# An unused tile of 640 bytes a partition in front of the FFN's tiles in SBUF

## The chip, the core and the metric

The kernel runs on one core of a Trainium2 chip, as one launch. The metric is the device time in microseconds of one execution. The profile is of a further execution of the same program; its instructions are timed by the hardware profiler, and its span runs from the first instruction's start to the last one's end.

## The reference, cut to what matters

Two layers over a residual stream x of 512 tokens by 1024 features, in float32. Each layer is an FFN at half weight, a mixing step with three groups of attention heads, and a second FFN at half weight:

```
for layer in range(2):
    h = modulate(rmsnorm(x), sh1, sc1)
    x = x + 0.5 * g1 * swiglu(h, w1[layer,0], w3[layer,0], w2[layer,0])
    ... mixing: projections, three kinds of attention, out projection
    h = modulate(rmsnorm(x), sh3, sc3)
    x = x + 0.5 * g3 * swiglu(h, w1[layer,1], w3[layer,1], w2[layer,1])
swiglu(h, w1, w3, w2) = (silu(h @ w1) * (h @ w3)) @ w2      # 1024 -> 2816 -> 1024
```

So there are four FFNs. The modulation (sh, sc, g) is computed from a conditioning vector with the weights `w_ada`.

## The kernel before, in words

Everything is kept with features on the 128 partitions and the 512 tokens along the free axis. To keep float32 accuracy on TensorE, each operand is split in two halves of type fp32r: a rounded part ("h" in `hh`, `gh`, `whi`) and the rest ("l" in `hl`, `gl`, `wlo`). A product of a block of weights (128 x 128, stationary) with a block of activations (128 x up to 512, moving) is then three matmuls that add up in PSUM (`mm3`, lines 309 to 311):

```
mm(out, l[0], r[0], start=start, stop=False, **kw)     # whi with hh or gh   L309
mm(out, l[0], r[1], start=False, stop=False, **kw)     # whi with hl or gl   L310
mm(out, l[1], r[0], start=False, stop=stop, **kw)      # wlo with hh or gh   L311
```

Weights come in pieces of 128 x 1024 float32 (eight blocks) through SyncE's DMA queue into `raw` (three buffers); ScalarE rounds a piece into `whi` (line 271) and VectorE subtracts for `wlo` (line 281), each with five buffers. They run ahead of TensorE until no buffer is free.

An FFN (function `ffn`) runs over two halves of 11 chunks of the 2816 hidden features. In the first part of a half, 8 blocks of w1 and 8 of w3 for each chunk go against the normed input `hh`, `hl` (eight chunks each). Silu and the product give `gf`, and ScalarE and VectorE split it into `gh` and `gl`. In the second part, for each of the eight chunks m of the output, the 11 blocks of w2 go against the 11 `gh`, `gl` of this half:

```
for j in range(HALF):
    wt = self.weight("ffn_w2", (l, f), hf * HALF + j, col(m))
    self.mm3(ps, wt, g[j], j == 0, j == HALF - 1)
```

The moving operand is 512 tokens wide, but in the second half's last two output chunks it is 256 wide (function `products`), so that the next norm can begin early. So an FFN has 14 whole output chunks (eight in the first half, six in the second) x 11 blocks x 3 = 462 matmuls of 512 columns on `gh` or `gl`, and 2 x 11 x 3 x 2 = 132 of 256 columns; the four FFNs have 1848 and 528.

Where the tiles lie in SBUF is settled when the program is built: pools are laid one behind the other, and a pool that is closed gives its room to the next. The constants, the weights (`raw`, `whi`, `wlo`), the activations (`hh`, `hl`) and small tiles come first and stay for the whole program. Behind them, from byte 113600 of each partition, lies either the FFN's pool (`fp`, opened by `open_ffn`) or the mixing's pool (`mp`). The FFN's pool holds `nt` (temporary of the norms), `sil`, `gf`, `gh`, `gl`, and, for the conditioning, `adaw` and `silc`. Byte addresses in a partition, as the built programs have them:

| tile | before | after | start modulo 512 before, after |
|---|---|---|---|
| `whi`, five of 4096 bytes | 36416 on | the same | 64, 64 (and each block of 128 columns in them) |
| `wlo`, five of 4096 bytes | 56896 on | the same | 64, 64 (and each block) |
| `hh`, eight of 2048 bytes | 77376 on | the same | 64, 64 |
| `hl`, eight of 2048 bytes | 93760 on | the same | 64, 64 |
| `gh`, fourteen at a time of 2048 bytes | 125888 on | 126528 on | 448, 64 |
| `gl`, fourteen at a time of 2048 bytes | 154560 on | 155200 on | 448, 64 |
| `nt`, `sil`, `gf`, `adaw`, `silc` | from 113600 | from 114240 | 448, 64 |
| `qk`, `att`, `tf` of the mixing's pool, `rmat` | 161344, 185920, 142912, 19520 on | the same | 64, 64 |

Modulo 2048 the tiles `hh`, `hl` start at 1600; `gh` and `gl` start at 960 before and at 1600 after.

Of the kernel before, what the change touches and what calls it, by code (L numbers as in the profile page):

```python
# [26 lines left out]
P = 128  # L27
# [36 lines left out]
def unit_sbuf(t, u):  # L64
# [4 lines left out]
SMALL = [("norm_g", (DEPTH * 3, KC), True),  # L69
         ("b_ada", (DEPTH, NMOD, KC), True), ("out_g", (DEPTH, KC), False), ("qk_g", (DEPTH, 4, RD), False),  # L70
         ("qk_gcol", (DEPTH, 4), False), ("rope", (2, NT, RD), False)]
HT = S // 2
HALVES = [slice(0, HT), slice(HT, S)]
TAIL = 2
# [108 lines left out]
class Net:  # L183
# [354 lines left out]

    def open_ffn(self, es):
        self.fp = es.enter_context(self.tc.tile_pool(name=self.name("fp"), bufs=1))  # L540
        self.temp = lambda: self.t(self.fp, "nt", [P, S], bufs=6)

    def open_ada(self):
# [112 lines left out]
    def unit_out(self, pair, u, z, att):  # L656

        nc = self.nc
        heads = range(2) if u == 0 else (u - 1,)
        outs = {e: z[:, HT * i:HT * i + HT] for i, e in enumerate(heads)}  # L660
        for i, (e, c, _, o, w) in enumerate(KEY_UNITS[u]):
            lhs = self.v[pair][:, c, e].rearrange("p a b -> p (a b)")
            for j, a in enumerate(att):
                nc.tensor.matmul(outs[e][:, HT - w:], lhs, a[:, o:o + w], start=i + j == 0,  # L664
                                 stop=c == KEY_UNITS[u][-1][1] and j == 1, skip_group_check=True)
# [3 lines left out]
        for e in heads:  # L669
            out = self.o[pair][HD * e:HD * e + HD, HT * (u > 0):HT * (u > 0) + HT]  # L670
            own, other = (outs[e][HD * i:HD * i + HD] for i in (e, 1 - e))
# [336 lines left out]
    def out_last(self, l):  # L1008
# [3 lines left out]
        for cs in HALVES:  # L1012
# [3 lines left out]
            order = [(c, m) for g in range(2) for c in range(4) for m in range(4 * g, 4 * g + 4)]  # L1016
            ps = lambda m: zs[m // 4][:, m % 4 * HT:m % 4 * HT + HT]
            for c, m in order:
# [140 lines left out]
```

## Time and profile before

| | |
|---|---|
| median of 3 runs | 2143.43 us (2143.17 to 2144.86) |
| the profiled execution: its own time | 2149.0 us |
| its span, first to last instruction | 2147.1 us |
| TensorE (PE) busy | 2096.4 us, 98% of the span |
| VectorE (DVE), ScalarE (ACT) busy | 60%, 39% |
| granted TensorE clock, mean | 0.996 of full speed |

The ends of matmuls in the profile are modelled, since they run in a pipeline: a row's duration for a matmul is longer than the time in which the next one follows. What a matmul costs in a stream of them is read as the distance from one start to the next, in the timeline. "PEld" rows are the loads of the stationary operand, which overlap the matmul before.

### The profile page before, as it was taken

What the parts mean: (1) busy time and instruction counts of PE and PEld (TensorE: products, weight loads), DVE (VectorE), ACT (ScalarE), POOL (GpSimd) and SP (SyncE); (2) the same over time, 40 slices, a digit from 0 to 9 for tenths busy, and PEclk for the clock granted to TensorE, in tenths of its full rate; (3) what the DMA queues carried; (4) which work ended last, traced back from release to release, by engine and by line L of the source; (5) the groups of instructions that cost most, each with busy time, mean ns of one, the idle gap of its engine ahead of it and who ended that gap; (6) DMA issues with size and microseconds to landing.
All of it is one profiled execution on the core that took longest, in us unless ns stands there. A gap on an engine that the chain in (4) does not pass through costs nothing.

```text
span 2147.1 us, 28606 instructions
## 1 busy us (share of the span) xinstructions
PE 2096.4 (98%) x11280; PEld 1806.7 (84%) x11280; DVE 1289.2 (60%) x2425; ACT 837.4 (39%) x1347; POOL 3.5 (0%) x12
## 2 busy tenths in 40 slices
PE   6999999999999999999999999999999999999999
PEld 5888888888998888888898888888889998888888
DVE  8772753679978777275374333346899776333332
ACT  3321222467675432122242222324776644222220
POOL 0000000000000000000000000000000000000000
PEclk9999999999999999999999999999999999999999
DMA  7783853342333378386334333324334223333331
GB/s 297 264 283 98 265 171 89 103 107 67 100 91 103 112 262 279 98 269 199 90 105 132 98 98 96 93 82 122 91 84 106 74 71 108 98 89 99 98 102 56
DMA packets 86149, 281.74 MB, mean 131 GB/s; under 512 B 10752, under 2 KB 13312, under 8 KB 86016
## 3 DMA queue, kind: packets, MB, share of 16 engines
q1 hardware_dynamic: 84576, 277.83, 42.3%
q8 instruction: 88, 1.44, 0.3%
q10 hardware_dynamic: 1440, 2.10, 0.3%
q14 instruction: 45, 0.37, 0.1%
HBM read 256.55 MB, written 2.10 MB: 120 GB/s over the span
## 4 chain that ended last, share of the span: by engine, by line
PE 84%; DVE 10%; ACT 3%; DMA 2%; issue 1%; SPq 0%; ACTq 0%; DVEq 0%
PE z L309 23%; PE z L311 23%; PE z L310 23%; PE b L309 3%; PE b L311 3%; PE b L310 3%; DVE sc L862 2%; DVE m L861 2%; PE z L620 1%; DVE att L575 1%; DMA qk<-qk 1%; DVE wlo L281 1%; PE z L664 1%; PE z L713 1%; DVE tf L725 1%
## 5 line engine op out<-in xcount | busy, mean ns | idle before, releaser
L281 DVE TENSOR_TENSOR wlo<-raw,whi 128x1024 fp32r<-128x1024 f32 (+1 forms) x338 | 412.4, 1221 | 534.0 <-ACT whi L271 532.0
L271 ACT CAST whi<-raw 128x1024 fp32r<-128x1024 f32 (+1 forms) x338 | 354.3, 1049 | 863.1 <-PE z L310 791.8
L309 PE MATMUL z<-hh,whi 128*128 128x512 f32 (+1 forms) x1616 | 597.6, 371 | 6.9 <-DVE xs L996 3.9
L310 PE MATMUL z<-hl,whi 128*128 128x512 f32 (+1 forms) x1616 | 597.5, 370 | 0.5
L311 PE MATMUL z<-hh,wlo 128*128 128x512 f32 (+1 forms) x1616 | 596.4, 370 | 1.3 <-DVE wlo L281 1.3
L309 PEld LDWEIGHTS z<-hh,whi 128*128 128x128 f32 x1616 | 306.4, 190 | 59.1 <-DVE xs L996 4.3
L311 PEld LDWEIGHTS z<-hh,wlo 128*128 128x128 f32 x1616 | 306.3, 190 | 52.6 <-DVE wlo L281 1.8
L310 PEld LDWEIGHTS z<-hl,whi 128*128 128x128 f32 x1616 | 306.5, 190 | 52.0 <-DVE hl L437 1.3
L309 PE MATMUL z<-gh,whi 128*128 128x512 f32 (+1 forms) x792 | 293.7, 371 | 0.0
L310 PE MATMUL z<-gl,whi 128*128 128x512 f32 (+1 forms) x792 | 292.9, 370 | 0.0
L311 PE MATMUL z<-gh,wlo 128*128 128x512 f32 (+1 forms) x792 | 289.2, 370 | 0.0
L356 DVE CUSTOM_DVE_ANT_0 adaw<-adaw,silc 128x1024 f32<-128x1024 f32 x144 | 170.9, 1222 | 30.0 <-DMA adaw<-in_w_ada_dram 29.9
L309 PEld LDWEIGHTS z<-gh,whi 128*128 128x128 f32 x792 | 148.9, 188 | 29.7
L311 PEld LDWEIGHTS z<-gh,wlo 128*128 128x128 f32 x792 | 149.0, 188 | 27.7
L310 PEld LDWEIGHTS z<-gl,whi 128*128 128x128 f32 x792 | 149.0, 188 | 26.5
L309 PE MATMUL b<-whi,hh 128*128 128x256 f32 x544 | 156.7, 288 | 3.0 <-DVE v L654 2.1
L311 PE MATMUL b<-whi,hl 128*128 128x256 f32 x544 | 154.7, 284 | 0.0
L310 PE MATMUL b<-wlo,hh 128*128 128x256 f32 x544 | 154.6, 284 | 0.0
L513 DVE SCALAR_TENSOR_TENSOR xs<-z,mod,xs 128x512 f32<-128x512 f32 (+1 forms) x72 | 49.7, 691 | 124.7 <-PE z L311 124.6
L309 PEld LDWEIGHTS b<-whi,hh 128*128 128x128 f32 x544 | 104.8, 193 | 4.0 <-PE b L311 2.4
L310 PEld LDWEIGHTS b<-wlo,hh 128*128 128x128 f32 x544 | 104.8, 193 | 0.2
L311 PEld LDWEIGHTS b<-whi,hl 128*128 128x128 f32 x544 | 104.6, 192 | 0.0
(146 smaller groups left out, 2242.9 us busy)
## 6 DMA issues: line engine op xcount, KB each, us to landing
raw<-in_w_dram SPq DMA_DIRECT2D x332, 512.0 KB, 3.6
adaw<-in_w_ada_dram SPq DMA_DIRECT2D x144, 512.0 KB, 4.8
qk<-qk SPq DMA_DIRECT2D x144, 128.0 KB, 2.3
qk<-qk SPq DMA_DIRECT2D x24, 96.0 KB, 3.3
xs<-in_x_dram SPq DMA_DIRECT2D x4, 512.0 KB, 5.2
raw<-in_w_dram SPq DMA_DIRECT2D x4, 492.0 KB, 3.5
silc<-in_c_dram SPq DMA_DIRECT2D x3, 512.0 KB, 5.1
out_dram<-xs ACTq DMA_DIRECT2D x6, 256.0 KB, 2.0
```

The costliest lines, as they stand in the source:

```text
L271: nc.scalar.copy(hi[:, :n], raw[:, :n])
L281: self.nc.vector.tensor_sub(lo[:, :n], raw[:, :n], hi.bitcast(F32)[:, :n])
L309: mm(out, l[0], r[0], start=start, stop=False, **kw)
L310: mm(out, l[0], r[1], start=False, stop=False, **kw)
L311: mm(out, l[1], r[0], start=False, stop=stop, **kw)
L356: r = self.nc.vector.tensor_tensor_reduce(w, w, self.silc, 1.0, 0.0, op0=ALU.mult, op1=ALU.add, accum_out=m[:, j:j + 1])
L513: nc.vector.scalar_tensor_tensor(self.x[m][:, cs], ps[:, cs], gate[:, m:m + 1], self.x[m][:, cs], op0=ALU.mult, op1=ALU.add)
L575: nc.vector.tensor_sub(unit_sbuf(lo, u), src, unit_sbuf(hi.bitcast(F32), u))
L620: self.nc.tensor.matmul(out, a, b, start=start and i == 0, stop=stop and i == 1, skip_group_check=True)
L664: nc.tensor.matmul(outs[e][:, HT - w:], lhs, a[:, o:o + w], start=i + j == 0, stop=c == KEY_UNITS[u][-1][1] and j == 1, skip_group_check=True)
L861: nc.vector.max(m8, sc)
L862: nc.vector.match_replace(sc, m8, sc, TAKEN)
```

## The change

One tile `shift` of 160 float32 a partition (640 bytes) is allotted as the first tile of the FFN's pool each time that this pool is opened. Nothing writes or reads it. Every other tile of that pool so lies 640 bytes higher; all tiles of the other pools stay where they are. The built programs have on each engine the same instructions in the same order with the same semaphore waits; they differ in the addresses of the FFN pool's tiles alone. The pool ends at byte 208448 at most, where it ended at 207808 before, so it still fits.

```diff
+SHIFT = 160
 ...
     def open_ffn(self, es):
         self.fp = es.enter_context(self.tc.tile_pool(name=self.name("fp"), bufs=1))
+        self.t(self.fp, "shift", [P, SHIFT])
         self.temp = lambda: self.t(self.fp, "nt", [P, S], bufs=6)
```

## Rows read from the trace of the kernel before

**Rows 1.** The page's first part: busy time, share of the span, instructions.

```profile
span 2147.1 us, 28606 instructions
PE 2096.4 (98%) x11280; PEld 1806.7 (84%) x11280; DVE 1289.2 (60%) x2425; ACT 837.4 (39%) x1347; POOL 3.5 (0%) x12
```

**Rows 2.** The page's chain that ended last, shares of the span by engine, by line.

```profile
PE 84%; DVE 10%; ACT 3%; DMA 2%; issue 1%; SPq 0%; ACTq 0%; DVEq 0%
```

**Rows 3.** Groups by line and shape: xcount, then busy us and mean ns.

```profile
L310 PE MATMUL z<-hl,whi 128*128 128x512 f32 x1296 | 505.3, 390 | 0.0
...
L310 PE MATMUL z<-gl,whi 128*128 128x512 f32 x616 | 243.2, 395 | 0.0
...
L310 PE MATMUL z<-gl,whi 128*128 128x256 f32 x176 | 49.6, 282 | 0.0
```

**Rows 4.** Timeline of PE in a first part: start us, duration us, instruction.

```profile
904.71 0.39 PE L309 MATMUL z<-hh,whi 128*128 128x512 f32 x1
904.94 0.39 PE L310 MATMUL z<-hl,whi 128*128 128x512 f32 x1
...
910.83 0.39 PE L309 MATMUL z<-hh,whi 128*128 128x512 f32 x1
```

**Rows 5.** Timeline of PE at both ends of a second part.

```profile
838.64 0.39 PE L310 MATMUL z<-hl,whi 128*128 128x512 f32 x1
838.86 0.39 PE L311 MATMUL z<-hh,wlo 128*128 128x512 f32 x1
839.09 0.40 PE L309 MATMUL z<-gh,whi 128*128 128x512 f32 x1
839.32 0.39 PE L310 MATMUL z<-gl,whi 128*128 128x512 f32 x1
839.55 0.40 PE L311 MATMUL z<-gh,wlo 128*128 128x512 f32 x1
839.79 0.39 PE L309 MATMUL z<-gh,whi 128*128 128x512 f32 x1
840.01 0.40 PE L310 MATMUL z<-gl,whi 128*128 128x512 f32 x1
...
892.65 0.39 PE L311 MATMUL z<-gh,wlo 128*128 128x512 f32 x1
892.88 0.40 PE L309 MATMUL z<-hh,whi 128*128 128x512 f32 x1
```

**Rows 6.** Busy time by stretch: stretch, length, engines (xcount), granted clock, DMA share, GB/s.

```profile
842.00:892.00 50.00, 50.00 (x217) 40.35 (x216) 20.56 (x25) 10.07 (x10) 0.00 (x0) 1.00 0.46 152
904.00:1020.00 116.00, 116.00 (x513) 96.06 (x512) 71.66 (x104) 33.27 (x41) 0.00 (x0) 1.00 0.69 226
```

**Rows 7.** Waits in 839 to 893 us: us in total, times, longest.

```profile
ACT whi L271 <- PE z L310: 42.7, 10, 6.7
DVE wlo L281 <- ACT whi L271: 19.2, 7, 5.1
DVE xs L513 <- PE z L311: 9.0, 4, 3.5
DVE adaw L356 <- DMA adaw<-in_w_ada_dram: 1.7, 2, 1.1
```

**Rows 8.** Timeline of PE in the 256-wide tail of a second half.

```profile
1067.66 0.28 PE L309 MATMUL z<-gh,whi 128*128 128x256 f32 x1
...
1069.91 0.28 PE L310 MATMUL z<-gl,whi 128*128 128x256 f32 x1
```

**Rows 9.** Timeline of PE in the out projection, 256 wide on `hh`, `hl`.

```profile
695.82 0.28 PE L309 MATMUL z<-hh,whi 128*128 128x256 f32 x1
...
698.46 0.28 PE L310 MATMUL z<-hl,whi 128*128 128x256 f32 x1
```

**Rows 10.** Timeline of PE in the mixing: merged rows and the row behind each.

```profile
434.87 0.98 PE L620 MATMUL z<-qk,qk 128*128 128x512 f32 x4
435.69 0.28 PE L309 MATMUL b<-whi,hh 128*128 128x256 f32 x1
...
586.06 1.16 PE L713 MATMUL z<-att,rmat 128*128 128x512 f32 x6
587.05 0.33 PE L309 MATMUL b<-whi,hh 128*128 128x256 f32 x1
```

**Rows 11.** Groups by line and shape on VectorE and ScalarE.

```profile
L437 DVE SCALAR_TENSOR_TENSOR hl<-nt,mod,hh 128x256 fp32r<-128x256 f32 x64 | 27.3, 481 | 2.2 <-ACT hh L436 2.1
...
L437 DVE SCALAR_TENSOR_TENSOR hl<-tf,mod,hh 128x256 fp32r<-128x256 f32 x16 | 6.9, 481 | 2.9 <-ACT hh L436 2.9
```

**Rows 12.** The page's DMA issues: xcount, KB each, median us to landing.

```profile
raw<-in_w_dram SPq DMA_DIRECT2D x332, 512.0 KB, 3.6
adaw<-in_w_ada_dram SPq DMA_DIRECT2D x144, 512.0 KB, 4.8
```

## The prediction

> **What bounds the kernel now.** I read the page's busy times first: TensorE is busy for 98% of the span, VectorE for 60%, ScalarE for 39% [rows 1]. The chain that ended last says the same: 84% of it is TensorE, 10% VectorE [rows 2]. So time that TensorE gains or loses in a long stretch of matmuls is, almost whole, time of the kernel. The stretch that concerns this change is the second part of each half of an FFN, where `gh` and `gl` stream against the w2 blocks, since these two are the only tiles of the FFN's pool that TensorE reads there. Its waits [rows 7] name nobody whom TensorE waits for: ScalarE and VectorE wait for TensorE to free `whi`, 42.7 us of 54, and the weights are there ahead of it.
>
> Next I looked at what one matmul costs. The groups by shape already show a difference that the code does not explain: 512 columns on `hl` have a mean of 390 ns, 512 columns on `gl` have 395 [rows 3]. The ends of these rows are modelled, so I went to the timeline and took distances from start to start. In a first part, on `hh` and `hl`: from 904.71 to 910.83 us are 27 steps, 6.12 / 27 = 226.7 ns each [rows 4]. In a second part, on `gh` and `gl`: from 839.09 to 892.88 us are 231 steps (all of them on `gh` or `gl`), 53.79 / 231 = 232.9 ns each [rows 5]. The change of pace falls on the very first `gh`: 838.64 to 838.86 to 839.09 are the regular steps, and then come 0.23, 0.23, 0.24, 0.22 in turn, which go on to the end.
>
> What could make two matmuls of equal shape differ by 6.2 ns? [...] The other engines don't explain it: in the first part VectorE is busy for 71.66 of 116 us and the DMA engines for 0.69, in the second for 20.56 of 50 us and 0.46, and the slower matmuls stand in the quieter stretch [rows 6]. The order in `mm3`, the stationary tiles and the PSUM tile `z` are the same. What remains is where the moving operand lies: `hh` and `hl` start at the same remainder modulo 512 bytes as every weight block (64), `gh` and `gl` at 448.
>
> **The change part by part.** No instruction, no wait and no transfer is added, removed or moved, so there is nothing to price but the addresses.
>
> *TensorE, 512 columns.* After the change `gh` and `gl` start at 64 modulo 512, and at 1600 modulo 2048, as `hh` and `hl` do. Their matmuls are then of the same form, with the same remainders, as those of [rows 4]. The trace has no `gh` at that place; the nearest row is `hh` at 226.7 ns, and it is near, since only the higher address bits differ. The eight `hh` and the five `whi` and `wlo` buffers already meet in many distances of whole 512 bytes without a change of pace. The gain is 1848 x (232.9 - 226.7) = 11.5 us. Its bounds: all of it, or nothing, if the place is not the cause.
>
> *TensorE, 256 columns.* Here the trace points the other way. In the tail `gh` runs from 1067.66 to 1069.91 us in 19 steps, 118.4 ns each [rows 8]; the out projection's `hh` from 695.82 to 698.46 in 22 steps, 120.0 ns each [rows 9]. If the tail takes the pace of `hh`, it loses 528 x 1.6 = 0.8 us. Its bounds are 0 and 0.8, and I take the loss.
>
> *VectorE and ScalarE.* Instructions that read a tile of the FFN's pool together with another (`nt` with `hh`) meet the new place too. The same line runs in the mixing with its temporary `tf`, which lies at 64 modulo 512 where `nt` lies at 448: both have 481 ns [rows 11]. So I price these at 0, with 0 on both sides.
>
> *DMA.* Only `adaw` and `silc` are loaded into that pool. `adaw` lands in 4.8 us where `raw`, as large and at remainder 64, needs 3.6 [rows 12]; that could be its place or its being issued in bursts. It is hidden either way: VectorE's waits for it are 1.7 us in 54 [rows 7], VectorE is off the path there, and the weights' loads are ahead. I take 0.
>
> *Sum.* 11.5 - 0.8 = 10.7 us less. The profiled execution took 2149.0 us with a span of 2147.1 [rows 1], 5.6 us above the median of the runs. The gain is a number of matmuls times a distance and doesn't hang on which execution one takes, so I subtract it from the median: 2143.4 - 10.7 = 2132.7 us, 0.50% less. Nothing else takes the bound over: in the first parts the same weights chain feeds TensorE at 226.7 ns a matmul while VectorE also does the conditioning, so it can feed the second parts at that pace.
>
> [...] The row says that equal shapes, at an equal clock, differ by 6.2 ns with the tile that is streamed [rows 4, 5]. [...]
>
> **The rivals.**
>
> *Place is not the cause (no change).* Something else in the second part, such as 11 blocks into one bank instead of 8, makes the matmuls slower, and stays: 2143.4 us. The onset at the first `gh` [rows 5] fits this too, as that is where the second part begins. Against it is that the uneven steps begin with the second matmul on `gh`, long before a group of 11 blocks is over. That equal remainders are not enough is a second form of it: four score products on `qk`, which lies at 64 like its stationary tile, take from 434.87 to 435.69 us [rows 10] for 1792 columns; at the pace of `hh` (13.3 ns over the columns' time) they would take 0.80, so each has about 5 ns more. If `gh` stayed 5 ns above `hh`, the gain would be 1848 x 1.2 = 2.2 us: 2141.2. Against this form is that those are short runs of mixed widths, and `gh` runs 198 or more in a row at one width.
>
> *Partial.* The irregular steps get shorter, but not to 226.7; halfway is a gain of 5.7 us: 2137.7.
>
> *Slower.* [...] The worst rows for operands at equal remainders are the stick-breaking products on `att` and `rmat`: six of 2048 columns together from 586.06 to 587.05 us [rows 10], 0.99 where 0.93 would be the pace of `hh`, about 9.5 ns more each. If `gh` ran so, 512 columns would cost 236.2 and 256 columns 129.5 ns: 1848 x 3.3 + 528 x 11.1 = 12.0 us more, 2155.4. It decides from a distance of 232.9 ns on. Against it are all the `hh` rows.
>
> **How the numbers follow.** 0.2% (4.3 us) is about what a measurement of this kernel can tell from no change. My forecast with the full pace of `hh` has 0.79, the partial one 0.06 (faster by over 0.2%, mostly), no change in either form 0.11, slower 0.04. So faster 0.85, same 0.11, slower 0.04. The predicted time is 2132.7. Around it the runs scatter by about 1 us, and the two terms may be off by some 10%. A range from 2130.0 up to the partial case, 2138.0, leaves out less than 2 in 10.
>
> **What the changed kernel's profile would show.** Right: in the second parts the steps on `gh` and `gl` are 226.7 ns and regular, the mean of the 512-column groups on `gl` falls from 395 to 390, the 256-column tail goes from 118.4 to 120, each half of an FFN with 264 such matmuls ends 1.6 us earlier against its start, and no group outside TensorE changes its mean by more than a few ns. Wrong: if the steps stay at 229 to 238 in turn, the place was not the cause; if they settle in another irregular rhythm, the remainder modulo 512 doesn't tell the whole; if they are regular and the kernel is not faster, something that I took as hidden came up, and the first place to look is what ends TensorE's idle time between the parts.

## The result and the profile after

| | before | after |
|---|---|---|
| median | 2144.14 us (4 runs, 2143.17 to 2145.4) | 2133.73 us (4 runs, 2131.62 to 2134.43) |
| the profiled execution, span | 2147.1 us | 2132.2 us |

The ratio is 0.9949 with a 95% interval of 0.9932 to 0.9967: the change makes the kernel 0.5% faster, by 10.4 us. In a second comparison (five runs of the change and nine of the kernel before) it was 2135.85 against 2145.74 us, ratio 0.9951 [0.9939, 0.9964], 9.9 us. The forecast was 2132.7.

The diff puts three lines into the file, so line 309 of before is 311 after, 310 is 312, 437 is 439. First the groups by line and shape of the changed kernel, the lines that answer to [rows 3] and [rows 11]; the columns are count, busy us and mean ns.

```profile
L312 PE MATMUL z<-hl,whi 128*128 128x512 f32 x1296 | 505.1, 390 | 0.0
...
L312 PE MATMUL z<-gl,whi 128*128 128x512 f32 x616 | 239.9, 390 | 0.0
...
L312 PE MATMUL z<-gl,whi 128*128 128x256 f32 x176 | 49.8, 283 | 0.0
...
L439 DVE SCALAR_TENSOR_TENSOR hl<-nt,mod,hh 128x256 fp32r<-128x256 f32 x64 | 27.3, 480 | 2.3 <-ACT hh L438 2.2
```

The group on `gl` went from 395 to 390 ns, the mean that `hl` has, and `hl` stayed. VectorE's instruction on `nt`, whose tile moved too, has 480 ns where it had 481.

Next the timeline of PE in the changed kernel around the start of the second part that [rows 5] shows for before, and 28 steps of the same part (start us, duration us, instruction).

```profile
832.14 0.39 PE L312 MATMUL z<-hl,whi 128*128 128x512 f32 x1
832.37 0.39 PE L313 MATMUL z<-hh,wlo 128*128 128x512 f32 x1
832.59 0.39 PE L311 MATMUL z<-gh,whi 128*128 128x512 f32 x1
832.82 0.39 PE L312 MATMUL z<-gl,whi 128*128 128x512 f32 x1
833.04 0.39 PE L313 MATMUL z<-gh,wlo 128*128 128x512 f32 x1
...
833.95 0.39 PE L311 MATMUL z<-gh,whi 128*128 128x512 f32 x1
...
840.30 0.39 PE L312 MATMUL z<-gl,whi 128*128 128x512 f32 x1
```

The first `gh` no longer breaks the pace: the steps go on as on `hh`. From 833.95 to 840.30 us are 28 steps, 226.8 ns each, where [rows 5] had 232.9.

One execution can mislead about the sum. The two spans differ by 14.9 us, half as much again as the medians. Here are stretches in which the granted clock was 0.50 or 0.51 in the profile of before, and then stretches near three of them in the profile of after (stretch, length, busy time of PE, PEld, DVE, ACT, POOL, granted clock, DMA share, GB/s).

```profile
397.00:400.40 3.40, 3.40 (x16) 3.39 (x15) 3.40 (x10) 2.34 (x6) 0.00 (x0) 0.51 0.40 146
458.50:461.90 3.40, 3.40 (x12) 2.92 (x11) 0.97 (x2) 1.87 (x2) 0.00 (x0) 0.50 0.32 72
717.90:721.30 3.40, 3.40 (x17) 3.40 (x18) 3.40 (x9) 1.95 (x5) 0.00 (x0) 0.50 0.01 5
```

```profile
396.00:400.00 4.00, 4.00 (x29) 4.00 (x28) 3.74 (x11) 3.01 (x6) 0.00 (x0) 1.00 0.04 11
457.00:461.00 4.00, 4.00 (x24) 3.35 (x22) 3.91 (x10) 2.04 (x3) 0.00 (x0) 1.00 0.01 4
716.00:721.00 5.00, 4.19 (x33) 3.74 (x33) 3.79 (x16) 0.00 (x0) 0.00 (x0) 1.00 0.35 108
```

The profile of before has five such stretches of 3.4 us at half clock, that of after two. In the stretch from 717.90 us the steps of 256 columns on `hh` and `hl` took 213 ns, where their mean over the whole profile is 119.9; in the one from 458.50 us 512 columns took 427 ns, where those on `hh` have 226.8. By these ratios 3.4 us at half clock did the work of 1.8 to 1.9 us, so, while TensorE is what the kernel waits for, the three that are missing are worth some 4.6 us, an estimate. 14.9 - 4.6 = 10.3 us is left, about what the medians show. The number of these stretches was between one and five in all profiles of this study, with and without a faster `gh`: four in the first experiment below, three and two in others of the same speed. It is scatter and no gain of the change. Runs of equal clock say the same: in the second comparison the four runs of the change with a mean granted clock of 0.998 took 2133.7 to 2135.9 us, and the two runs of the kernel before with that clock 2145.0 and 2145.2 us.

### The profile page after: what moved, and what is told of

It is laid out like the page before. It is cut to its first block, busy times and chain, and to the rows that moved or that the text cites. A ratio compares the mean times of both kernels' runs of the same rounds, so it can differ in the third digit from the quotient of the medians.

```text
span 2132.2 us, 28606 instructions
## 1 busy us (share of the span) xinstructions
PE 2081.8 (98%) x11280; PEld 1800.9 (84%) x11280; DVE 1288.7 (60%) x2425; ACT 837.7 (39%) x1347; POOL 3.0 (0%) x12
## 4 chain that ended last, share of the span: by engine, by line
PE 83%; DVE 12%; ACT 3%; DMA 2%; issue 1%; SPq 0%; ACTq 0%; DVEq 0%
PE z L311 23%; PE z L313 23%; PE z L312 23%; PE b L311 3%; PE b L313 3%; PE b L312 3%; DVE sc L865 2%; DVE m L864 2%; DVE wlo L283 2%; DVE att L578 1%; PE z L623 1%; PE z L667 1%; DMA qk<-qk 1%; DVE tf L728 1%; ACT tf L770 1%
## 5 line engine op out<-in xcount | busy, mean ns | idle before, releaser
L273 ACT CAST whi<-raw 128x1024 fp32r<-128x1024 f32 (+1 forms) x338 | 354.8, 1050 | 852.1 <-PE z L312 782.5
L311 PE MATMUL z<-hh,whi 128*128 128x512 f32 (+1 forms) x1616 | 596.7, 370 | 7.0 <-DVE xs L999 3.9
L311 PEld LDWEIGHTS z<-hh,whi 128*128 128x128 f32 x1616 | 305.6, 189 | 59.1 <-ACT hh L438 4.4
L311 PE MATMUL z<-gh,whi 128*128 128x512 f32 (+1 forms) x792 | 291.1, 368 | 0.0
L311 PEld LDWEIGHTS z<-gh,whi 128*128 128x128 f32 x792 | 149.3, 189 | 27.5 <-DVE xs L515 0.7
L311 PE MATMUL b<-whi,hh 128*128 128x256 f32 x544 | 156.5, 288 | 3.0 <-DVE v L657 2.1
L311 PEld LDWEIGHTS b<-whi,hh 128*128 128x128 f32 x544 | 104.6, 192 | 4.0 <-PE b L313 2.4
```

What stands on the lines that cost most here:

```text
L273: nc.scalar.copy(hi[:, :n], raw[:, :n])
```

## The experiments

The question for all of them is how long a step (start to start) on `gh`, `gl` and on `hh`, `hl` is, and what sets it. The mean step is worked out from the timeline of each run: all distances between successive starts on these tiles, without those over 60 ns above the columns' own time (waits). That own time is put at 0.417 ns a column, an estimate from `hh`'s paces in [rows 4] and [rows 9]: (226.7 - 120.0) / 256; it leaves 13.3 ns a matmul. "Distance" is the moving tile's start minus the stationary block's start, modulo 256 bytes; that 256 is the right number is what the runs with 384 and 256 bytes showed.

| kernel | distance of `gh` | `gh`, 512 wide | `gh`, 256 wide | `hh`, 512 wide | time, us |
|---|---|---|---|---|---|
| before | 128 | 232.8 ns (1844 steps) | 118.9 ns (516) | 226.8 ns (3876) | 2144.1 |
| the change, 640 bytes | 0 | 227.2 | 119.8 | 226.7 | 2133.7 |
| weights moved to `gh` | 0 | 227.2 | 119.8 | 226.7 | 2135.4 |
| 128 bytes | 0 | 227.1 | 119.8 | 226.7 | 2135.6, one run |
| 384 bytes | 0 | 227.1 | 119.8 | 226.7 | 2135.7, one run |
| 256 bytes | 128 | 232.8 | 118.6 | 226.8 | 2142.4, one run |
| 64 bytes | 192 | 233.3 | 115.8 | 226.7 | 2143.4, one run |
| 160 bytes | 32 | 233.3 | 116.8 | 226.8 | 2144.7, one run |
| 192 bytes | 64 | 229.2 | 116.9 | 226.8 | 2136.2, one run |
| `hh` moved away too | 128 | 232.6 | 118.9 | 232.8 (at 128 as well) | 2168.3 |

The kernel before, run beside them, was at 2145.0 us (weights moved, 128, 384 and 256 bytes) and at 2144.8 us (the other four).

**Weights moved to `gh`.** The theory of the prediction is that two starts have to agree; the rival is that a tile's own place is good or bad. Here `gh` and `gl` lie where they lay before, at 448 modulo 512, and the weights and `hh`, `hl` are moved to 448. The diff is against the kernel before:

```diff
+        self.sp = ctx.enter_context(tc.tile_pool(name="tiny", bufs=1))
         self.wp = ctx.enter_context(tc.tile_pool(name="weights", bufs=1))
         self.hp = ctx.enter_context(tc.tile_pool(name="acts", bufs=1))
-        self.sp = ctx.enter_context(tc.tile_pool(name="tiny", bufs=1))
```

> The FFN's pool stays where it was before the change (gh and gl at 448 modulo 512); the pool of tiny tiles is laid ahead of the weights instead, so that whi, wlo, hh and hl move up by 3456 bytes, to 448 modulo 512. Theory one (what counts is the moving operand's start against the stationary block's, modulo 512): all are equal again, so gh and hh both step at 226.7 ns at 512 columns, and the time is that of the change, about 2133.5 us. Theory two (what counts is the moving tile's own start, 64 is good and 448 is bad): gh stays at 232.9 and hh becomes 232.9 as well, 3888 x 6.2 = 24 us more than before, about 2168. Theory three (neither, the second part of an FFN is slow by itself and the change helped by something else): gh stays at 232.9, hh at 226.7, 2144.

Measured: 2135.38 us against 2145.03, ratio 0.9956 [0.994, 0.9973]. In its groups by line and shape both tiles have the shorter mean:

```profile
L310 PE MATMUL z<-hl,whi 128*128 128x512 f32 x1296 | 505.1, 390 | 0.0
...
L310 PE MATMUL z<-gl,whi 128*128 128x512 f32 x616 | 240.1, 390 | 0.0
```

That is theory one. No tile of the FFN's pool was moved, so the gain of the change is not one of `adaw`, `nt` or the other tiles of that pool; and the second part of an FFN is not slow by itself.

**128, 384 and 256 bytes instead of 640.** Each is the change with another `SHIFT` (32, 96, 64 floats), to find what has to agree.

> The unused tile has 128 bytes: gh and gl start at 64 modulo 512 but at 1088 modulo 2048, not at 1600 as hh does. If the remainder modulo 512 is what counts, steps on gh are 226.7 ns and the time is about 2133.5 us. If the remainder modulo 1024 or 2048 counts, the steps are irregular and between 228 and 241 ns, and the time is about 2144.

> The unused tile has 384 bytes: gh and gl start at 320 modulo 512, which is 64 modulo 256, as the weight blocks do. If the remainder modulo 256 is what counts, steps on gh are 226.7 ns and the time is about 2133.5 us. If it is modulo 512, the steps stay irregular, some 230 to 236 ns on average, and the time is within 5 us of 2144.

> The unused tile has 256 bytes: gh and gl start at 192 modulo 512, 128 behind the weight blocks. Under modulo 256 this is the same as before the change: 232.9 ns on average with the same alternation of 229 and 238, 2144 us. Under modulo 512 it is another distance: irregular too, with a rhythm of its own, mean between 228 and 238 ns, 2135 to 2153 us. Steady steps of 226.7 ns here would speak against both.

Measured: 128 bytes and 384 bytes give the whole gain (227.1 ns; 2135.63 and 2135.7 us), 256 bytes none (232.8 ns, 2142.4 us). So it is the remainder modulo 256 that has to agree; I had spoken of 512. With 384 bytes `gh` starts at 320 modulo 512, where the weight blocks start at 64, and the steps are those of the change. Each of the three times is of a single run; the steps are counted over some 1840 matmuls. The group on `gl` with 384 bytes, and then with 256:

```profile
L312 PE MATMUL z<-gl,whi 128*128 128x512 f32 x616 | 239.9, 389 | 0.0
```

```profile
L312 PE MATMUL z<-gl,whi 128*128 128x512 f32 x616 | 243.3, 395 | 0.0
```

**`hh` moved away too.** If the cause is right, the cost can be doubled and more at will. The pool of tiny tiles is put between the weights and the activations, so that `hh` and `hl` too are 128 off the weight blocks:

```diff
         self.wp = ctx.enter_context(tc.tile_pool(name="weights", bufs=1))
+        self.sp = ctx.enter_context(tc.tile_pool(name="tiny", bufs=1))
         self.hp = ctx.enter_context(tc.tile_pool(name="acts", bufs=1))
-        self.sp = ctx.enter_context(tc.tile_pool(name="tiny", bufs=1))
```

> The pool of tiny tiles is laid between the weights and the activations: whi and wlo stay at 64, hh and hl go to 448 modulo 512 (128 from the weight blocks modulo 256), gh and gl stay at 448. If the distance of moving and stationary start modulo 256 sets the pace, hh takes the pace that gh has: 232.8 ns at 512 columns, in the first parts (3888 matmuls) and the mixing's projections (624), 4512 x 6.1 = 27.5 us more; the 256-column ones on hh and those with whi as moving operand (2592) become about 1.2 ns shorter, 3.1 us less. Together about 24 us more than before: 2168.5. If only gh or the second part of an FFN is sensitive, 2144.

Measured: 2168.33 us against 2144.81, ratio 1.0106 [1.0089, 1.0123]; 23.5 us slower where 24 were expected. The groups by line and shape:

```profile
L310 PE MATMUL z<-hl,whi 128*128 128x512 f32 x1296 | 511.9, 395 | 0.0
...
L310 PE MATMUL z<-gl,whi 128*128 128x512 f32 x616 | 243.2, 395 | 0.0
```

Now `hl` has the 395 ns that `gl` had before, in the same instructions at the same places of the program.

**Other distances: 64, 160 and 192 bytes.** Again the change with another `SHIFT` (16, 40, 48 floats), for distances of 192, 32 and 64.

> The unused tile has 64 bytes: gh and gl start 192 behind the weight blocks modulo 256. If only equal starts give the steady pace, 512-column steps on gh are irregular, near 232.8 ns on average (2144 us). If the distance matters by degrees, they lie between 226.7 and 232.8. If some distances are better than 0, below 226.7.

> The unused tile has 160 bytes: gh and gl start 32 behind the weight blocks modulo 256. If only equal starts give the steady pace, steps near 232.8 ns (2144 us). If the distance matters by degrees, closer to 226.7 than with 64 bytes (about 2135 us). Below 226.7 if a small lead is better than none.

> The unused tile has 192 bytes: gh and gl start 64 behind the weight blocks modulo 256, the mirror of 192. If only the distance counts and not its sign, the same steps as with the tile of 64 bytes. If what counts is who leads, another pace.

Measured: 192 and 32 are as slow at 512 columns as 128 (233.3 ns); 64 lies between (229.2 ns). So the pace is not a matter of degrees from 0, since 32 is worse than 64, and 64 and 192 are not mirrors of each other. No distance beat 0 at 512 columns. At 256 columns it is the other way: 0 is the slowest of all with 119.8 ns, and 192 the fastest with 115.8. The timeline of the run with 64 bytes in the tail (19 steps from the first to the last row, 2.15 us, 113.2 ns each in this stretch) answers to [rows 8], where 19 steps took 2.25:

```profile
1067.81 0.28 PE L311 MATMUL z<-gh,whi 128*128 128x256 f32 x1
...
1069.96 0.28 PE L312 MATMUL z<-gl,whi 128*128 128x256 f32 x1
```

**128 bytes between `whi` and `wlo`.** This asks which stationary block has to agree, the matmul's own or the one that is loaded beside it. The diff is against the kernel before, in `load_piece`:

```diff
+        if not self.gap:
+            self.gap = self.t(self.wp, "gap", [P, 32])
         lo = self.t(self.wp, "wlo", [P, 1024], F32R, bufs=5)
```

> The kernel before with 128 unused bytes between the whi and the wlo buffers, so that all that lies behind them moves up by 128: gh and gl are now at whi's remainder modulo 256 and 128 off wlo's, while hh and hl are at wlo's and 128 off whi's. In a row of three matmuls two stationary loads are whi, one is wlo. If each step is delayed or not by itself, according to the load that runs beside it, gh has two good steps of three (mean 228.7 ns at 512 columns) and hh one of three (230.8), and the time is about 2144 - 7.6 + 18.5 = 2155. If one unequal load is enough to break the steady rhythm for all, both are at 232 to 233 ns, about 2171. If only the tile's own stationary block counts, L311 alone is off on gh and L309 and L310 on hh.

Measured: 2170.98 us (one run). The mean steps on `gh`, `gl`: 227.7 ns from L309's start to the next, 232.2 from L310's, 234.3 from L311's. On `hh`, `hl`: 232.6, 232.5 and 235.0. Six steps in a second part of this run (L309 is 312 here, L310 313, L311 314; rows are start us, duration us, instruction):

```profile
860.03 0.39 PE L312 MATMUL z<-gh,whi 128*128 128x512 f32 x1
860.26 0.40 PE L313 MATMUL z<-gl,whi 128*128 128x512 f32 x1
860.49 0.40 PE L314 MATMUL z<-gh,wlo 128*128 128x512 f32 x1
860.73 0.39 PE L312 MATMUL z<-gh,whi 128*128 128x512 f32 x1
860.95 0.40 PE L313 MATMUL z<-gl,whi 128*128 128x512 f32 x1
861.18 0.40 PE L314 MATMUL z<-gh,wlo 128*128 128x512 f32 x1
861.42 0.39 PE L312 MATMUL z<-gh,whi 128*128 128x512 f32 x1
```

No form of the expectation got it whole. The time is that of "one unequal load breaks all"; the steps are not. On `gh`, whose start agrees with `whi` alone, the one good step in three is the one whose own block and whose next load are both `whi`; the step that has `wlo` next and the step that has `wlo` as its own are both slow. On `hh`, which agrees with `wlo` alone, no step has `wlo` twice, and none is good. So the block that is loaded for the next matmul mattered here: in the step from L310's start (232.2 ns) its own block agrees and the step before it is a good one (227.7), and only `wlo`, which comes next, is off. The load of the next block starts with the matmul ahead of it: in the profile of before L309 on `gh` starts at 1030.57 us and the load for L310 at 1030.58. That the matmul's own block matters too is not shown: the slow step from L311's start stands behind a slow one, and in the changed kernel too the steps behind a disturbed place stay slow for a while (see "512 columns" below). One run cannot separate the two.

A rival that no run tests by itself is that `gh` should agree with the places into which ScalarE, VectorE and the DMA write the weights meanwhile, and not with the block that TensorE reads. The steps of this run speak against it, since they change from matmul to matmul within a row of three (227.7, 232.2 and 234.3 ns) with the block that is used. (In this run the mixing's tiles also moved by 128 against the constants, which touches its short products, not these steps.)

**A version for the 256-wide matmuls.** Since 256 columns had their shortest steps at a distance of 192 (115.8 ns against 119.8 at 0), I gave the change a lead in `whi` for the pieces whose matmuls are 256 wide, so that the moving operand starts 192 bytes behind the stationary one (modulo 256), and ran it beside the change itself. To make room for the longer tiles the program is built with `dynamic_dma_scratch_size` 32, where it was 1024.

```diff
+def lead(piece):
+    name, _, _, ranges = PIECES[piece][0]
+    n = sum(b - a for a, b in ranges)
+    return 0 if name not in ("w_in", "w_out") else 48 if n == 256 else 16 if n == D else 0
...
-        hi = self.t(self.wp, "whi", [P, 1024], F32R, bufs=5)
+        hi = self.t(self.wp, "whi", [P, 1024 + 64], F32R, bufs=5)
+        hi = hi[:, lead(self.piece):]
```

> The change, and on top of it the whi tiles are 1088 columns long instead of 1024, and a piece whose matmuls are 256 columns wide is put behind a lead, so that the moving operand starts 192 bytes behind the stationary one modulo 256 (mixing projections, whi moving: 48 columns; out projection's last part, whi stationary: 16 columns). The wlo tiles stay. At distance 192 the tail's 256-column steps took 115.8 ns, against 119.8 at distance 0. If this holds there, 1088 + 512 matmuls gain up to 4 ns, 6.3 us at most: 2127 to 2131 where the change alone is at 2133.5. If the rhythm needs wlo to agree too, or the mixing is bound by VectorE where it matters, within 2 us of the change. If mixed distances break the rhythm, slower than the change by up to 2 us.

> The change as it is, on the same chip as the run with the lead, for a direct comparison: 0.5% under the kernel before, 2132 to 2136 us.

Measured: 2134.19 us with the lead (five runs, 2131.64 to 2136.32; ratio to before 0.9946 [0.9932, 0.9959]) and 2135.85 us for the change alone (ratio 0.9951 [0.9939, 0.9964]). The intervals lie on each other: no difference that this measures. TensorE did get shorter steps there: 118.1 ns on average for the matmuls with weights as 256-wide moving operand against 119.7, and 119.1 against 119.9 on `hh`. Its busy time in the page's first part is 4.2 us shorter:

```profile
PE 2078.6 (98%) x11280; PEld 1797.6 (84%) x11280; DVE 1288.2 (60%) x2425; ACT 836.8 (39%) x1347; POOL 3.5 (0%) x12
```

```profile
PE 2082.8 (98%) x11280; PEld 1802.4 (85%) x11280; DVE 1288.7 (60%) x2425; ACT 837.6 (39%) x1347; POOL 3.5 (0%) x12
```

The first line is of the version with the lead, the second of the change measured beside it. Not all of the 4.2 us is the lead's: that profile has two stretches of 3.4 us at half clock and the other three, and one such stretch is worth some 1.5 us by the ratios above. The steps alone make some 3 us (1566 x 1.6 ns and some 900 x 0.8 ns), and the medians differ by 1.7 us, less than these runs can tell from nothing. With `wlo` left at distance 0 the steps fell by about 1.6 ns and not by 4. Whether a lead for `wlo` too would give the rest was not tried.

## Why the prediction was right, point by point

**What bounds the kernel.** TensorE's steps were the path: the steps got shorter by the sum below and the time fell by as much. The chain that ended last has TensorE at 83% after, 84% before. The granted clock was 1.00 in both stretches of [rows 6], so it is not what sets 226.7 and 232.9 ns apart. The waits of the FFN's second parts did not change hands: in the waits of the whole changed kernel ScalarE still waits 782.5 us for TensorE to free `whi`.

```profile
ACT whi L273 <- PE z L312: 782.5, 240, 6.7
DVE wlo L283 <- ACT whi L273: 526.2, 204, 6.1
```

**512 columns.** Forecast 1848 x (232.9 - 226.7) = 11.5 us. Measured over all steps: 1848 x (232.8 - 227.2) = 10.3 us. After a wait, or where the third matmul of a row of three is out of its place, the pace is not at once at 226.7: in the profile of after 155 of the 1840 steps take 230 ns or more, 233.1 on average, and 154 of these lie within ten steps behind such a place. They hold the mean at 227.2; the other 1685 average 226.7, the forecast pace. From its first to its last matmul of 512 columns the second part with 264 of them went from 62.4 to between 60.9 and 61.1 us, where 1.6 us less was forecast, and the one with 198 from 47.0 to 45.9 us.

**256 columns.** Forecast a loss of 0.8 us from two rows; over all steps it is 528 x (119.8 - 118.9) = 0.5 us. The sign was right, and the experiments show that it belongs to distance 0 and not to the tile: the 256-wide steps on `hh` went from 119.9 to 118.6 ns when `hh` was moved away.

**Sum.** 10.3 - 0.5 = 9.8 us from the steps; 10.4 and 9.9 us from the medians. The forecast of 10.7 was 0.9 us above the steps' sum: the gain at 512 columns was put 1.2 us too high, mostly (0.9) by the slow steps just named, and the loss at 256 columns 0.3 us too high. That these two partly cancel is luck, but neither is large.

**VectorE, ScalarE, DMA at nothing.** The group on `nt` went from 481 to 480 ns, and `adaw` still lands in 4.8 us (median), at its new place; its longer landing beside `raw` is then not a matter of its start's remainder.

**What was imprecise.** The prediction took the remainder modulo 512 as the measure, since `hh` and the weights agreed there. What has to agree is the remainder modulo 256; 640 bytes satisfy both, so the forecast did not depend on it. The rivals: "place is not the cause" falls with the run in which the weights came to `gh`, and with the one in which `hh` became slow. "Partial" exists, but at a distance of 64 (229.2 ns). "Slower" at equal starts did not come; the slowest of the distances has 233.3 ns, half a nanosecond more than before. Its price was misread from [rows 10]: of the six products on `att` the first step takes 292 ns, and the other five together 707 ns for 1536 columns, which is the pace of `hh` carried over to other widths (640 for the columns at 0.417 ns and five times 13.3). The 13.3 ns a matmul of the prediction is the one that [rows 4] and [rows 9] give (2 x 120.0 - 226.7); that it holds at 128 and 384 columns too is an estimate. What was spread over six matmuls as 9.5 ns each is one long step, so those rows were no sign against equal starts. The four products on `qk` have steps of 233, 236, 172 and 179 ns, 6 to 9 ns above the pace but for the third; why was not tested. Nor does `gh` run 198 or more in a row, as the prediction says against this form of "no change": the rows are of 231, 33, 165 and 33 matmuls, with others between them. That is still long enough for the argument.

**What stays open.** With `hh` moved away the same 3888 matmuls went from 226.8 to 232.8 ns when nothing but addresses had changed, so the place of an operand counts here. What in SBUF or TensorE makes the two starts matter stays open; the runs show which distances are good, and one run that the block being loaded counts.

## What to carry to other kernels

In a kernel that is bound by long runs of matmuls with a new stationary block each, compare the start-to-start distance of equal shapes between stages; a stage that is slower at the same clock, with no wait (here 232.8 against 226.8 ns, 2.6%), is worth a look at where its operands lie. Here 512-column fp32r matmuls had their shortest steps where the moving tile and the stationary block start at the same remainder modulo 256 bytes (227.2 ns against 229.2 to 233.3), and in its one run an unused tile of 128 bytes gave as much as the 640 (227.1 ns); at 256 columns the same distance was the slowest (119.8 ns against 115.8 to 118.9). Check this again whenever a small tile is added ahead of a pool, since it can cost as much: `hh` moved away cost 23.5 us. Take the gain from medians: in this kernel one profile differs from another by up to four stretches of 3.4 us at half clock.

## What the runs showed of the hardware that I had not expected

- Starts that differ by 256 bytes alone gave the same pace (640 and 384 bytes, none and 256), and the good distance at 512 columns is exactly 0 among 0, 32, 64, 128 and 192: 227.2, 233.3, 229.2, 232.8 and 233.3 ns.
- At 256 columns the order turns round: 119.8, 116.8, 116.9, 118.9 and 115.8 ns (the fourth has 118.9 in two runs and 118.6 in a third).
- At distance 0 the steps are even in long runs (226 to 228 ns). At the others they follow rhythms: at distance 64 three steps such as 226, 229 and 232 ns, at 32 often four (231, 235, 233, 234), at 128 often two (229 and 238), but in some stretches seven (232, 228, 230, 233, 241, 232, 231), with nearly the same mean.
